# Attention: full softmax weights kept in PSUM over their scores, and their sum split between GpSimd and TensorE

## The chip, the cores and the metric

The kernel runs on one core of one Trainium2 chip. The metric is the device time of one launch in microseconds (us). The core has TensorE for matrix products (PE in the rows, PEld for its weight loads), VectorE (DVE), ScalarE (ACT), GpSimd (POOL) and SyncE (SP), which only issues DMAs here. Each engine takes its instructions strictly in the order in which they were built and waits on semaphores for the others.

## The reference

One step of a four-layer network over 1024 latent and 128 context tokens of 1024 channels: Hyena, latent attention (MLA), RWKV-7, Hyena. The change touches the attention of the second layer alone. For each of 16 heads it computes

```
s = einsum('bqhd,bkhd->bhqk', qn, k_nope) + einsum('bqhr,bkr->bhqk', qp, k_pe)
p = softmax(s * 96 ** -0.5, axis=-1)
o = einsum('bhqk,bkhd->bqhd', p, v)          # then  (o * silu(z)) @ w_out
```

where the 1024 latent queries see 1280 keys (256 cached, 1024 own) and the 128 context queries see 128 keys. Head width is 64 plus 32 positional channels, values are 64 wide.

## The kernel before, in words

Products are made at nearly full precision from split operands: a value x is kept as a rounded high part and a low part x - high, and a product is high*high + high*low + low*high.

Scores are computed transposed, keys on partitions and queries on columns, in **tiles** of 128 keys by 512 queries. A head has 21 tiles: ten key blocks for queries 0 to 511, ten for queries 512 to 1023 (each ten is a **group**), and one small tile, 128 by 128, for the context. For a tile, `scores` issues three products into a PSUM bank (L1459 to L1461). The first has a 97th row, which subtracts each query's maximum. `attend` then lets ScalarE read the bank twice: `exp` in full into a tile `pf` (L1492, for the first tile of a group straight into the sum `sm`) and `exp` rounded into `wh` (L1493). VectorE subtracts them into the low part `wl` (L1497), GpSimd adds `pf` to the group's running sum `sm` (L1499). `values` multiplies both parts with the values, [v_hi | v_lo] side by side in 128 columns, into one bank `ps_pv` (L1466, L1467). Tiles `pf`, `wh` and `wl` come from rings of four, so that ScalarE can be four tiles ahead of the last reader of a ring.

`finish` follows each group: the low half of `ps_pv` is copied (L1517) and added to the high half (L1519), the columns of `sm` are summed over partitions on TensorE (L1523), inverted (L1525), spread, transposed (L1534) and multiplied in with the gate (L1536, L1537).

Beside head h run `maxima(h + 1)` and `head_prep(h + 2)`. `maxima` takes 25 products of queries by keys (L1436, eight times 512, 512 and 256 columns, once 128), each reduced to row maxima on VectorE (L1437), then L1440 and L1441, a transpose (L1443), a copy `mr` on ScalarE (L1445), and a DMA that writes the maxima into row 96 of the queries `qh` (L1446). No score of a head can start before that DMA has landed. `head_prep` makes keys, queries and values of later heads (L262 to L264 into `ps_pj`, with ScalarE copies and VectorE subtractions).

PSUM has eight banks. In this stage `set_banks` gives three in turn to maxima and projections (`pj`), one to `fn`, two to the scores (`st`) and two to `pv`. A scheduler sets the order of instructions on each engine when the kernel is built; the steps of `weave` are only its input.

Of the kernel before, what the change touches and what calls it, by code (L numbers as in the profile page):

```python
# [20 lines left out]
P = 128  # L21
# [111 lines left out]
def rwkv_constants():  # L133
# [19 lines left out]
    # of each level's mask the columns that change, for four chunks of each direction  # L153
# [69 lines left out]
class Prog:  # L223
# [22 lines left out]
    def set_banks(self, **kinds):  # L246
        """Which PSUM banks each kind of product (or several kinds together) takes, in turn."""
# [22 lines left out]
    def load_split(self, hi, lo, src, lo_eng=None, pool=None):  # L270
        """DRAM [1024, n <= 128] -> split [128, KC, n], through a staging tile, in two halves."""
# [18 lines left out]
    def mod_part(self, i, part):  # L290
        """Columns (part * 512 ...) of silu(cond) @ mod_w[i] + mod_b[i], for both conditions."""
# [40 lines left out]
    def mod_fast(self, i):  # L332
        """Shift and scale of both conditions on the tensor engine; 16 steps."""
# [30 lines left out]
    def fold_mod(self, i):  # L364
        """h = xn * G + B with xn the normalised rows (or x itself before the first layer)."""
# [21 lines left out]
    def next_group(self, i):  # L387
        """Room for another group of tokens of layer i's input; the RWKV layer takes it unsplit."""
# [6 lines left out]
    def emit_h(self, i, t, xn, pool):  # L395
        """Token tile t of xn (token-major) -> modulated, channel-major, split in hh / hl (or in h32)."""
# [72 lines left out]
    def load_w(self, src):  # L469
        """src [1024, 128]: split weights, k-chunks along the free axis."""  # L470
# [26 lines left out]
    def boundary(self, i, w_out, y_src, last):  # L497
        """x <- LN(alpha x + gate * (y @ w_out)); y_src(t) loads token tile t as [128, KC, 128], split."""
# [3 lines left out]
        with tc.tile_pool(name="bd", bufs=1, reuse_waits="tile") as pool:  # L502
# [23 lines left out]
            def load_x(t):  # L526
                """alpha x, kept as that after the first layer."""
# [66 lines left out]
    def wout_half(self, w_out, half, turns=True):  # L594
        """Half the columns of w_out, split, in a pool at the far end of the memory; four steps."""
# [11 lines left out]
    def norm_stats(self, s, pool):  # L607
        """Mean and 1 / deviation of every row, in columns 0 and 2."""
# [12 lines left out]
    def load_cst(self, r, k, pool, bufs, raw=False):  # L621
        """DFT constants, split; from the given ones the first time."""
# [14 lines left out]
    def fw_mats(self, r, t):  # L637
        """(re->re, im->re, re->im, im->im) as (hi, lo) pairs."""
# [3 lines left out]
    def stage1_odd(self, xo, out, pool, w):  # L642
        """Odd outputs of the 16-point DFT of eight values; out(r, part)."""
# [4 lines left out]
        # real  # L648
# [14 lines left out]
        # imaginary  # L663
# [16 lines left out]
    def stage1_even(self, xe, out, pool, w):  # L680
        """Even outputs of the 16-point DFT of eight values."""
# [31 lines left out]
    def stage1_inv(self, u, out, pool, w):  # L713
        """u(r, part) -> out(a), a in 0..7 (the inverse of the residues)."""
# [87 lines left out]
    def sine(self, ps, w, freq, fb, y, k):  # L802
        """sin(freq * ps + fb) with the argument reduced to [-pi, pi]."""
# [12 lines left out]
    def features(self, j, pool, fd):  # L816
        """Hidden features of the implicit filter at all positions, split, one block for each pair of taps."""
# [42 lines left out]
    def filters(self, j, pool):  # L860
        """Spectra of the two-sided filter (plus the skip at lag 0), unit by unit -> DRAM."""
# [14 lines left out]
        def weights(q):  # L876
            """Output weights of the filter network, decays and skip of unit q."""
# [91 lines left out]
    def hyena(self, i, j, lead, rest):  # L969
        """lead: steps that come before the first product with h; rest: steps to be done by the end."""  # L970
# [12 lines left out]
        def conv3(col, dst, then):  # L983
            """Job: three-tap convolution of u column tile `col` into dst() [128, W] (a spare column at LS)."""
# [46 lines left out]
        def jobs_gate(b):  # L1031
            """conv3(x0) * silu(z) -> DRAM."""
# [29 lines left out]
        def blocks(q, pool):  # L1062
            """Time blocks of v * x1, token-major."""
# [133 lines left out]
    def mla(self, i, rest):  # L1197
        """rest: steps to be done by the end."""
# [42 lines left out]
        def latents():  # L1241
            """Queries' and keys' compressed forms, token-major -> normalised, channel-major, split."""
# [61 lines left out]
        def early():  # L1304
            """What needs no room of the layer's input."""
# [25 lines left out]
        def pair_values(p):  # L1331
            """Values of a pair of heads, token-major: [v_hi | v_lo] of each head side by side."""
            wk, vv = pairs[p][0], self.big([P, NK, 2, 2, 64], "vv")
            pairs[p].append(vv)
            for t0 in range(0, NK, 4):
                n = min(4, NK - t0)
# [6 lines left out]
                dst = vv[:, t0:t0 + n].rearrange("p t a b n -> p t (a b) n")  # L1343
                nc.scalar.copy(dst[:, :, 0:4:3], src)
                nc.vector.tensor_tensor(dst[:, :, 1:3], src, dst[:, :, 0:4:3], ALU.subtract)
# [16 lines left out]
        def turn(u):  # L1362
            """Positional parts of the queries of four heads, 32 rows each."""
# [28 lines left out]
        def head_prep(h):  # L1392
            """Keys and queries of a head."""
# [55 lines left out]
        rings = [[self.mp.tile([P, 512], F32, tag=tag, name="pf", bufs=n) for tag, n in  # L1449
                  (("macc0", 1), ("macc1", 1), ("modw", 2), ("modw", 2))]]  # L1450
# [13 lines left out]
        def values(h, t, first, last, pv, ph, pl, done):  # L1464
            vl = pairs[h // 2][1][:, t, h % 2].rearrange("p a n -> p (a n)")
            nc.tensor.matmul(pv, vl, ph, start=first, stop=False)  # L1466
            nc.tensor.matmul(pv, vl, pl, start=False, stop=last)  # L1467
            if last:
                later.append([1, finish(h, *done)])

        def attend():
            """All heads' softmax and weighted values, 42 steps each."""
# [3 lines left out]
            due = []  # L1476
            for i, (h, q0, nq, t, first, last) in enumerate(tiles):
                if h % 2 and first:
# [11 lines left out]
                if first:  # L1490
                    pf = sm
# [70 lines left out]
        for x in later:  # L1562
            weave(x[1])
# [770 lines left out]
```

## Time and profile before

| what | before |
|---|---|
| median of three runs | 4658.84 us (4657.1 to 4663.7) |
| span of the profiled execution, first to last instruction | 4633.9 us |
| between that span and the median of the runs | 24.9 us |
| attention stage, 1160 to 1856 us of the span: PE, DVE, ACT, POOL busy | 649.1, 647.8, 463.0, 546.0 of 696 us |
| granted TensorE clock in the stage | 0.97 of full speed |

The span is what the trace covers; the time of a run is a little longer. Busy time of PE overlaps itself (ends of products are modelled), so PE is read by the distance between starts.

### The profile page before, as it was taken

The page shows a single profiled execution, that of the slowest core. Times are in us where ns is not written, and L with a number is a line of the kernel's source. Part 1 is how long each engine was busy: PE and PEld are TensorE (multiplying, and loading weights), DVE is VectorE, ACT ScalarE, POOL GpSimd, SP SyncE. Part 2 cuts the span into 40 slices and gives each one's busy share as a digit, 9 for nine tenths or more (in the row PEclk, how much of TensorE's full clock was granted, in tenths as well). Part 3 has the DMA queues.
Part 4 walks back from the last instruction along what each step waited for, and adds up shares of the span by engine and source line. Part 5 has one row for each costly group of instructions (what it writes and reads, how often), then busy time and mean ns, then how long its engine had stood idle before and what let it go on. Part 6 is the DMA issues. An engine that isn't in the chain of part 4 may idle for free. (4 is left out here: it accounts for less than half of the span.)

```text
span 4633.9 us, 81733 instructions
## 1 busy us (share of the span) xinstructions
PE 4125.1 (89%) x29736; PEld 3562.3 (77%) x29736; DVE 3545.7 (77%) x6307; ACT 2395.0 (52%) x5468; POOL 2358.6 (51%) x1902
## 2 busy tenths in 40 slices
PE   7988988989999998978989777999999889988998
PEld 4888888778777776767877566888888678978986
DVE  6777887655999999587578996777777568967877
ACT  5654433554676676344455544666566456643331
POOL 3655766343787787355546652233333233476550
PEclk8999999988999999989978886999899899989999
DMA  5755455543000001436635462222222423764445
GB/s 174 241 181 174 156 158 171 185 135 98 18 17 24 26 15 39 137 130 196 176 116 184 163 228 74 59 79 71 77 72 65 136 95 113 222 202 151 144 151 181
DMA packets 490975, 582.90 MB, mean 126 GB/s; under 512 B 59819, under 2 KB 378333, under 8 KB 489933
## 3 DMA queue, kind: packets, MB, share of 16 engines
q1 hardware_dynamic: 489068, 576.70, 39.7%
q8 instruction: 235, 3.85, 0.3%
q14 instruction: 168, 1.37, 0.1%
q10 hardware_dynamic: 1504, 0.98, 0.1%
HBM read 413.74 MB, written 161.37 MB: 124 GB/s over the span
## 5 line engine op out<-in xcount | busy, mean ns | idle before, releaser
L262 PE MATMUL ps_mm<-hh,wh 128*128 128x384 f32 x1728 | 594.3, 345 | 47.6 <-ACT hh L267 24.0
L263 PE MATMUL ps_mm<-hl,wh 128*128 128x384 f32 x1728 | 592.8, 343 | 2.6 <-DVE hl L268 1.6
L264 PE MATMUL ps_mm<-hh,wl 128*128 128x384 f32 x1728 | 591.8, 343 | 0.0
L1499 POOL TENSOR_TENSOR sm<-sm,pf 128x512 f32<-128x512 f32 x288 | 443.1, 1539 | 115.4 <-DVE wl L1497 37.3
L268 POOL TENSOR_TENSOR wl<-wraw,wh 128x512 fp32r<-128x512 f32 x212 | 331.2, 1580 | 182.5 <-ACT wh L267 170.1
L262 PEld LDWEIGHTS ps_mm<-hh,wh 128*128 128x128 f32 x1728 | 334.0, 194 | 56.2 <-ACT hh L267 25.1
L1497 DVE TENSOR_TENSOR wl<-pf,wh 128x512 fp32r<-128x512 f32 x288 | 352.1, 1232 | 7.9 <-ACT wh L1493 7.6
L263 PEld LDWEIGHTS ps_mm<-hl,wh 128*128 128x128 f32 x1728 | 333.9, 193 | 7.6 <-DVE hl L268 4.3
L264 PEld LDWEIGHTS ps_mm<-hh,wl 128*128 128x128 f32 x1728 | 333.8, 193 | 3.3 <-issue 3.3
L2139 POOL TENSOR_TENSOR tot<-SV,wcs 64x128 f32<-64x128 f32 x288 | 114.7, 405 | 391.6 <-DVE SV L2167 360.6
L305 POOL TENSOR_TENSOR macc<-macc,mprod 128x512 f32<-128x512 f32 x140 | 212.3, 1517 | 172.3 <-ACT mprod L304 139.6
L263 PE MATMUL ps_mm<-mx,wh 128*128 128x384 f32 x680 | 254.6, 375 | 35.1 <-DVE mx L1669 34.0
L262 PE MATMUL ps_mm<-mx,wh 128*128 128x384 f32 x680 | 257.3, 380 | 13.9 <-ACT mx L1668 5.7
L262 PE MATMUL ps_mm<-woh,hh 128*128 128x512 f32 x576 | 235.8, 411 | 33.8 <-ACT hh L267 31.0
L264 PE MATMUL ps_mm<-mx,wl 128*128 128x384 f32 x680 | 249.3, 368 | 3.7 <-POOL wl L268 3.7
L1492 ACT ACTIVATE pf<-ps_st 128x512 f32<-128x512 f32 x288 | 172.4, 599 | 143.4 <-POOL sm L1499 57.5
L264 PE MATMUL ps_mm<-woh,hl 128*128 128x512 f32 x576 | 234.5, 407 | 2.9 <-DVE hl L268 2.8
L263 PE MATMUL ps_mm<-wol,hh 128*128 128x512 f32 x576 | 232.2, 403 | 0.1
L1437 DVE TENSOR_REDUCE mx<-ps_pj 128x1 f32<-128x512 f32 (+2 forms) x400 | 220.0, 574 | 13.4 <-PE ps_pj L1436 12.6
L302 DVE SCALAR_TENSOR_TENSOR macc<-modw,cond,macc 128x512 f32<-128x512 f32 x140 | 156.4, 1118 | 92.8 <-DMA modw<-mod_w 92.1
L304 ACT ACTIVATE mprod<-modw,cond 128x512 f32<-128x512 f32 x140 | 101.3, 724 | 197.3 <-POOL macc L305 109.3
L1493 ACT ACTIVATE wh<-ps_st 128x512 fp32r<-128x512 f32 x336 | 194.3, 578 | 0.0
(560 smaller groups left out, 13314.6 us busy)
## 6 DMA issues: line engine op xcount, KB each, us to landing
cst<-cst SPq DMA_DIRECT2D x175, 384.0 KB
modw<-mod_w SPq DMA_DIRECT2D x160, 256.0 KB
wraw<-hy_w_in SPq DMA_DIRECT2D x128, 256.0 KB
kd<-kt SPq DMA_DIRECT2D x72, 384.0 KB
kt<-kd SPq DMA_DIRECT2D x72, 384.0 KB
cst<-cst SPq DMA_DIRECT2D x41, 512.0 KB
ctd<-ct SPq DMA_DIRECT2D x24, 768.0 KB
bkd<-bk SPq DMA_DIRECT2D x24, 768.0 KB
```

The source lines that it names most:

```text
L262: mm(ps, lh, rh, start=start, stop=False)
L263: mm(ps, lh, rl, start=False, stop=False)
L264: mm(ps, ll, rh, start=False, stop=stop)
L268: (lo_eng or self.nc.gpsimd).tensor_tensor(lo, src, hi, ALU.subtract)
L302: nc.vector.scalar_tensor_tensor(acc[0], w, s, acc[0], op0=ALU.mult, op1=ALU.add)
L305: nc.gpsimd.tensor_tensor(acc[1], acc[1], wp, ALU.add)
L1437: nc.vector.tensor_reduce(mx[:, t, j:j + 1], ps, AX.X, ALU.max)
L1492: nc.scalar.activation(pf, s, AF.Exp, scale=scale)
L1493: nc.scalar.activation(ph, s, AF.Exp, scale=scale)
L1497: nc.vector.tensor_tensor(pl, pf, ph, ALU.subtract)
L1499: nc.gpsimd.tensor_tensor(sm, sm, pf, ALU.add)
L2139: g_.tensor_tensor(tot[h], SV[e][h, jsl], wc[h].unsqueeze(2).broadcast_to([64, 2, 64]), M)
```

## The change

The full weights are no longer written to SBUF. ScalarE writes the rounded weights `wh` first and then overwrites the scores in their own PSUM bank with the full weights; VectorE subtracts `wh` from that bank. The ring of `pf` goes. GpSimd's running sum adds the rounded parts `wh` only. The sum of the low parts comes from TensorE: the values get 32 columns of ones between their parts (288 columns a key block for two heads: lo, hi, ones, hi, lo), and the product of the low part takes hi and ones, while that of the high part takes lo and hi. The two products now accumulate in two PSUM regions, `a` and `b`. `finish` copies both halves of `a` (L1543, L1544), copies the row of ones' sums (L1546), adds `b` on VectorE (L1547), and two more additions on GpSimd join the sums (L1549) and the output (L1550). The last key block's values live in a small tile of their own (`vl`). Banks are dealt anew: maxima, projections and `fn` share two, the scores have three, `pv` three.

```diff
-            wk, vv = pairs[p][0], self.big([P, NK, 2, 2, 64], "vv")
+            wk, vp = pairs[p][0], self.big([P, NK - 1, 288], "vv")
+            last = self.mp.tile([P, 1, 288], F32R, tag=f"macc{p % 2}", name="vl", bufs=1)
...
+                nc.gpsimd.tensor_copy(x[:, :, 128:160], self.ones[:, :32].unsqueeze(1).broadcast_to([P, n, 32]))
...
-                nc.vector.tensor_tensor(dst[:, :, 1:3], src, dst[:, :, 0:4:3], ALU.subtract)
+                for e in range(2):
+                    nc.vector.tensor_tensor(dst[:, :, e * 224:e * 224 + 64], src[:, :, e], hi[:, :, e], ALU.subtract)
...
-            nc.tensor.matmul(pv, vl, ph, start=first, stop=False)
-            nc.tensor.matmul(pv, vl, pl, start=False, stop=last)
+            nc.tensor.matmul(g["a"], pairs[h // 2][1][t][:, c0:c0 + P], ph, start=first, stop=last)
...
+            nc.tensor.matmul(g["b"], pairs[h // 2][1][t][:, c0:c0 + P], pl, start=first, stop=last)
...
-                nc.scalar.activation(pf, s, AF.Exp, scale=scale)
-                nc.scalar.activation(ph, s, AF.Exp, scale=scale)
+                    nc.scalar.activation(ph, s, AF.Exp, scale=scale)
+                    nc.scalar.activation(s, s, AF.Exp, scale=scale)
...
-                nc.vector.tensor_tensor(pl, pf, ph, ALU.subtract)
-                if not first:
-                    nc.gpsimd.tensor_tensor(sm, sm, pf, ALU.add)
+                    nc.vector.tensor_tensor(pl, s, ph, ALU.subtract)
...
+                        nc.gpsimd.tensor_tensor(g["sm"], before if t == 1 else g["sm"], p32, ALU.add)
...
-            nc.scalar.copy(au[mrow], pv[arow])
+            nc.scalar.copy(au[mrow], g["a"][arow])
+            nc.scalar.copy(oT[mrow, qs], g["a"][mrow])
...
-            nc.vector.tensor_tensor(oT[mrow, qs], pv[mrow], au[mrow], ALU.add)
+            nc.scalar.copy(au[srow], g["b"][srow])
+            nc.vector.tensor_tensor(au[mrow], g["b"][mrow], au[mrow], ALU.add)
+            yield False
+            nc.gpsimd.tensor_tensor(sm[srow], sm[srow], au[srow], ALU.add)
+            nc.gpsimd.tensor_tensor(oT[mrow, qs], oT[mrow, qs], au[mrow], ALU.add)
...
-        self.set_banks(pj=(0, 1, 2), fn=(5,), st=(3, 4), pv=(6, 7))
+        self.set_banks(pj_fn=(0, 1), st=(2, 3, 4), pv=(5, 6, 7))
```

The scheduler also orders the stage differently. First place: TensorE at the end of the sixth head, before the change, from the head's last scores (the small tile). L1443 is the transpose of the next head's maxima; the next head's first scores stand six rows behind this piece.

```order
L1459 MATMUL ps_st<-qh,kh_10355 128x128
L1460 MATMUL ps_st<-qh,kh_10355 128x128
L1461 MATMUL ps_st<-qh,kh_10355 128x128
L1466 MATMUL ps_pv<-wh,vv 128x512
L1443 MATMUL ps_pj<-ident,mn 9x128
L1467 MATMUL ps_pv<-wl,vv 128x512
L1466 MATMUL ps_pv<-wh,vv 128x512
L1467 MATMUL ps_pv<-wl,vv 128x512
L1523 MATMUL ps_fn<-ones,sm 128x1 x4
L1466 MATMUL ps_pv<-wh,vv 128x128
L262 MATMUL ps_pj<-qTh,wqu 128x384
L263 MATMUL ps_pj<-qTl,wqu 128x384
```

The same place after the change, from the eleventh row behind the head's last scores on. L1441 is the product of the maxima (L1436 before), L1448 their transpose, L1554 the sums of `sm`; the next head's first scores (L1463) stand eight rows behind this piece.

```order
L1441 MATMUL ps_pj<-kh_10353,qh 128x512 x2
L1441 MATMUL ps_pj<-kh_10353,qh 128x256
L1441 MATMUL ps_pj<-kh_10353,qh 128x512 x2
L262 MATMUL ps_pj<-cTh,wku 64x384
L263 MATMUL ps_pj<-cTl,wku 64x384
L264 MATMUL ps_pj<-cTh,wku 64x384
L1441 MATMUL ps_pj<-kh_10353,qh 128x256
L1441 MATMUL ps_pj<-kh_10353,qh 128x512 x2
L1441 MATMUL ps_pj<-kh_10353,qh 128x128
L1441 MATMUL ps_pj<-kh_10353,qh 128x256
L1554 MATMUL ps_fn<-ones,sm 128x1 x4
L1448 MATMUL ps_pj<-ident,mn 9x128
```

Before, all products of the next head's maxima stood ahead of the head's last scores; now thirteen of the 25 stand behind them (three of these ahead of the piece), and the transpose behind those.

Second place: VectorE at the end of the same head after the change. L1518 is the subtraction of weights (L1497 before), L1442 the reduction of a maxima product, L1547 the addition of `finish`, L1445 and L1446 the last steps of the maxima.

```order
L1518 TENSOR_TENSOR wl<-ps_st,wh 128x512
L1442 TENSOR_REDUCE mx<-ps_pj 128x1
L1518 TENSOR_TENSOR wl<-ps_st,wh 128x128
L1442 TENSOR_REDUCE mx<-ps_pj 128x1 x2
L1547 TENSOR_TENSOR au<-ps_pv,au 64x512
L1547 TENSOR_TENSOR au<-ps_pv,au 64x128
L1442 TENSOR_REDUCE mx<-ps_pj 128x1 x6
L1394 TENSOR_TENSOR kh_10354<-ps_pj,kh_10354 64x384
L1442 TENSOR_REDUCE mx<-ps_pj 128x1 x3
L1446 TENSOR_SCALAR mn<-mx 128x1
L1442 TENSOR_REDUCE mx<-ps_pj 128x1
L1445 TENSOR_REDUCE mn<-mx 128x8
```

Before, the steps L1440 and L1441 of the next head's maxima stood ahead of the subtraction of the small tile; now twelve reductions follow it.

## Rows read from the trace of the kernel before

**Rows 1.** The page's busy time, its share of the span and instructions of each engine.

```profile
PE 4125.1 (89%) x29736; PEld 3562.3 (77%) x29736; DVE 3545.7 (77%) x6307; ACT 2395.0 (52%) x5468; POOL 2358.6 (51%) x1902
```

**Rows 2.** Windows: length, PE, PEld, DVE, ACT, POOL busy, clock, DMA share, GB/s.

```profile
1160.00:1856.00 696.00, 649.08 (x2994) 497.61 (x2992) 647.83 (x940) 462.95 (x932) 545.99 (x379) 0.97 0.08 24
```

**Rows 3.** Instructions of line L1459: duration min/median/max, first and last start.

```profile
L1459 PE MATMUL ps_st<-qh,kh x336: 222/398/774, 1158.3 to 1850.9; 97*128 97x512 f32 x160, 97*128 97x128 f32 x8
```

**Rows 4.** Groups by form, DVE, 1160 to 1856: count | busy us, mean ns | idle.

```profile
L1497 DVE TENSOR_TENSOR wl<-pf,wh 128x512 fp32r<-128x512 f32 x288 | 352.1, 1232 | 7.9 <-ACT wh L1493 7.6
...
L1497 DVE TENSOR_TENSOR wl<-sm,wh 128x512 fp32r<-128x512 f32 x32 | 25.6, 800 | 1.6 <-ACT wh L1493 1.2
...
L1389 DVE TENSOR_TENSOR kh<-ps_pj,kh 64x512 fp32r<-64x512 f32 x28 | 18.9, 675 | 6.8 <-ACT kh L1388 6.8
```

**Rows 5.** Timeline, DVE, 1357 to 1361: start us, duration us.

```profile
1357.06 0.67 DVE L1497 TENSOR_TENSOR wl<-sm,wh 128x512 fp32r<-128x512 f32 x1
1357.66 0.67 DVE L1497 TENSOR_TENSOR wl<-pf,wh 128x512 fp32r<-128x512 f32 x1
...
1358.93 0.67 DVE L1519 TENSOR_TENSOR oT<-ps_pv,au 64x512 f32<-64x512 f32 x1
...
1360.12 2.16 DVE L1497 TENSOR_TENSOR wl<-pf,wh 128x512 fp32r<-128x512 f32 x1
```

**Rows 6.** Timeline, POOL, the same stretch.

```profile
1357.87 1.63 POOL L1499 TENSOR_TENSOR sm<-sm,pf 128x512 f32<-128x512 f32 x1 [2.49 <-ACT q L1412]
1359.46 1.01 POOL L268 TENSOR_TENSOR qh<-qe,qh 96x384 fp32r<-96x384 f32 x1
1360.44 1.29 POOL L1499 TENSOR_TENSOR sm<-sm,pf 128x512 f32<-128x512 f32 x1
```

**Rows 7.** Groups by form, POOL, 1160 to 1856.

```profile
L1499 POOL TENSOR_TENSOR sm<-sm,pf 128x512 f32<-128x512 f32 x288 | 443.1, 1539 | 115.4 <-DVE wl L1497 37.3 <-ACT pf L1492 36.3 <-DVE ri L1525 11.9
```

**Rows 8.** Groups by form, ACT, 1160 to 1856.

```profile
L1492 ACT ACTIVATE pf<-ps_st 128x512 f32<-128x512 f32 x288 | 172.4, 599 | 143.4 <-POOL sm L1499 57.5 <-PE ps_st L1461 43.0 <-issue 26.5
```

**Rows 9.** Waits, 1160 to 1856: us in total, times, longest us.

```profile
PEld ps_pv L1467 <- DVE wl L1497: 83.8, 127, 2.6
...
PEld ps_pj L1436 <- DVE mx L1437: 9.7, 26, 1.2
```

**Rows 10.** Timeline, PE, around the ends of heads: start us, duration us.

```profile
1197.70 0.23 PE L1459 MATMUL ps_st<-qh,kh 97*128 97x128 f32 x1
...
1201.76 0.44 PE L1459 MATMUL ps_st<-qh,kh 97*128 97x512 f32 x1
...
1283.07 0.23 PE L1459 MATMUL ps_st<-qh,kh 97*128 97x128 f32 x1
...
1290.21 0.27 PE L1443 MATMUL ps_pj<-ident,mn 128*9 128x128 f32 x1
...
1293.79 0.50 PE L1459 MATMUL ps_st<-qh,kh 97*128 97x512 f32 x1
...
1294.36 0.39 PE L1461 MATMUL ps_st<-qh,kh 96*128 96x512 f32 x1
1294.59 0.40 PE L1459 MATMUL ps_st<-qh,kh 97*128 97x512 f32 x1
...
1810.61 0.22 PE L1459 MATMUL ps_st<-qh,kh 97*128 97x128 f32 x1
...
1817.25 0.77 PE L1459 MATMUL ps_st<-qh,kh 97*128 97x512 f32 x1
```

**Rows 11.** Timeline, DVE, at the head's end of 1283 us.

```profile
1288.99 0.15 DVE L1441 TENSOR_SCALAR mn<-mx 128x1 f32<-128x1 f32 x1
```

**Rows 12.** Timeline, ACT, at the same head's end.

```profile
1284.51 0.30 ACT L1493 ACTIVATE wh<-ps_st 128x128 fp32r<-128x128 f32 x1
...
1291.40 0.26 ACT L1445 CAST mr<-ps_pj 9x128 fp32r<-9x128 f32 x1
```

**Rows 13.** Timeline, SP (its DMA issues), at the same head's end.

```profile
1291.69 0.79 SPq L1446 DMA_DIRECT2D qh<-mr  x1
```

More of the change, by code (lines that the diff above doesn't have):

```diff
@@ L1331, in pair_values @@
         def pair_values(p):
[L1333 to L1336 removed]
+            wk, vp = pairs[p][0], self.big([P, NK - 1, 288], "vv")
+            last = self.mp.tile([P, 1, 288], F32R, tag=f"macc{p % 2}", name="vl", bufs=1)
+            pairs[p].append([vp[:, t] for t in range(NK - 1)] + [last[:, 0]])
+            for x in (vp, last):
+                n = x.shape[1]
+                nc.gpsimd.tensor_copy(x[:, :, 128:160], self.ones[:, :32].unsqueeze(1).broadcast_to([P, n, 32]))
+            for t0, n in ((0, 4), (4, 4), (8, 2), (NK - 1, 1)):
                 ps = self.psum("pj")
@@ L1448, in mla @@
         later = []
-        rings = [[self.mp.tile([P, 512], F32, tag=tag, name="pf", bufs=n) for tag, n in
-                  (("macc0", 1), ("macc1", 1), ("modw", 2), ("modw", 2))]]
+        rings = []
         for tag in ("wh", "wl"):
@@ L1462, in scores, with values_hi, values_lo @@
             return s
-        def values(h, t, first, last, pv, ph, pl, done):
-            vl = pairs[h // 2][1][:, t, h % 2].rearrange("p a n -> p (a n)")
-            nc.tensor.matmul(pv, vl, ph, start=first, stop=False)
-            nc.tensor.matmul(pv, vl, pl, start=False, stop=last)
-            if last:
-                later.append([1, finish(h, *done)])
+        def values_hi(g, t, first, last, ph):
+            h, nq = g["h"], g["nq"]
+            if first:
+                bank = self.psum("pv")
+                g["a"] = bank[:, :nq]
+                if nq == P:
+                    g["b"] = bank[:, P:2 * P]
+            c0 = h % 2 * 160
+            nc.tensor.matmul(g["a"], pairs[h // 2][1][t][:, c0:c0 + P], ph, start=first, stop=last)
+            if last:
+                later.append(finish(g))
+        def values_lo(g, t, first, last, pl):
+            h, nq = g["h"], g["nq"]
+            if "b" not in g:
+                g["b"] = self.psum("pv")[:, :nq]
+            c0 = 64 + h % 2 * 32
+            nc.tensor.matmul(g["b"], pairs[h // 2][1][t][:, c0:c0 + P], pl, start=first, stop=last)
         def attend():
@@ new lines, in attend @@
+            his, los = [], []
+            for i in range(len(tiles) + 3):
+                if i < len(tiles):
+                    h, q0, nq, t, first, last = tiles[i]
+                    if h % 2 == 0 and q0 == 0 and first:
+                        oT = outs[:, h // 2 % 2]
+                        ri = pool2.tile([P, 2, NT], F32, tag="ri", name="ri", bufs=2)
+                    if first:
+                        sz = None
+                        if h % 2:
+                            sz = pool2.tile([P, 512], F32, tag="szl", name="szl", bufs=2)[:, :nq]
+                            nc.sync.dma_start(sz, szd[h // 2, :, q0:q0 + nq])
+                        g = dict(h=h, q0=q0, nq=nq, sz=sz, oT=oT, ri=ri,
+                                 sm=pool2.tile([P, 512], F32, tag="sm", name="sm", bufs=3)[:, :nq])
+                    s = ahead.pop(0)
+                    ph, pl = (x[i % 4][:, :nq] for x in rings)
+                    nc.scalar.activation(ph, s, AF.Exp, scale=scale)
+                    nc.scalar.activation(s, s, AF.Exp, scale=scale)
+                if his:
+                    values_hi(*his.pop(0))
+                if len(los) > 1 or (los and i >= len(tiles)):
+                    values_lo(*los.pop(0))
+                yield
+                if i < len(tiles):
+                    nc.vector.tensor_tensor(pl, s, ph, ALU.subtract)
+                    p32 = ph.bitcast(F32)
+                    if first and last:
+                        nc.gpsimd.tensor_copy(g["sm"], p32)
+                    elif not first:
+                        nc.gpsimd.tensor_tensor(g["sm"], before if t == 1 else g["sm"], p32, ALU.add)
+                    before = p32
+                    if i + 2 < len(tiles):
+                        ahead.append(scores(*tiles[i + 2]))
+                    his.append((g, t, first, last, ph))
+                    los.append((g, t, first, last, pl))
@@ L1503, in attend, with finish @@
                 for x in list(later):
-                    x[0] -= 1
-                    if x[0] < 0 and next(x[1], True):
+                    if next(x, True):
                         later.remove(x)
-                if last and q0 == LS:
+                if i < len(tiles) and last and q0 == LS:
                     del qhs[h]
                 yield
-            values(*due.pop())
-        def finish(h, q0, nq, pv, sm, sz, oT, ri):
+        def finish(g):
+            h, q0, nq, sm, sz, oT, ri = (g[x] for x in ("h", "q0", "nq", "sm", "sz", "oT", "ri"))
```

31 lines of the change are left out of this document (6 added, 25 removed).

## The prediction

> **What bounds the kernel now.** The page comes first: PE is busy in 89% of the span and nothing else in more than 77% [rows 1], so the whole kernel has no single bound and the change must be judged in its stage. The attention lies between the first and the last scores, 1158.3 and 1850.9 us [rows 3]: 692.6 us, 43.3 a head. There the windows show PE at 649 and DVE at 648 of 696 us, POOL at 546, ACT at 463 [rows 2]. PE's busy time overlaps itself. Full-size products start 0.23 us apart, as at 1294.36 and 1294.59 [rows 10], and by that distance (in proportion for narrower ones, 0.11 for those of 128 columns) all products between first and last scores sum to 559 us: PE has over 130 us to spare. DVE has none to speak of, and PE waits for it: 83.8 us for `wl` in the longest wait [rows 9].
>
> Why DVE is full stands in the groups by form. The subtraction of weights takes 1232 ns on average, while a subtraction of the same width that takes one operand from PSUM takes 675 [rows 4]. The timelines show what lengthens it: at 1357.66 it takes 0.67 us, and GpSimd's addition which starts inside it ends late (1.63 against 1.29). At 1360.12 it starts inside GpSimd work, lasts 2.16 us, and ends half a microsecond after the next GpSimd addition has ended at 1361.73; the VectorE addition from PSUM at 1358.93 keeps its 0.67 beside both [rows 5, 6]. So a subtraction with two SBUF operands and a GpSimd addition exclude each other, and one with a PSUM operand does not.
>
> The stage has a second part: between a head's last scores and the next head's first. These gaps last 4.06 us at the first of 15 heads' ends and 6.64 at the last, 10.72 at the longest but one that I follow here [rows 10]; together 83.0 us. Hence 609.6 us, or 38.1 a head, are spent between first and last scores of heads.
>
> **The change, part by part.** *The subtraction* now reads PSUM: 288 times 1232 becomes 675, 32 times 800 becomes 675 [rows 4], 164 us less DVE work. *GpSimd's additions* go from 1.54 [rows 7] to 1.29 [rows 6] and 0.08 us of handover, 48 us less; but `finish` brings two full-width ones for each of 32 groups, at 1.29 (a row of one partition is priced as a full one, bounds 0.1 and 1.3), and small ones for the 16 context tiles: 100 us more with the ones. GpSimd so comes to 600 us, 37 a head. *ScalarE* gets 37 us of copies, hidden in 233 idle us [rows 2]; if that cover were gone they would cost 2.3 us a head. Overwriting scores in PSUM is not in the trace; I take the 0.6 us of the exp into SBUF [rows 8], bounds 0.5 and 0.7, which by 320 is 32 us either way on an engine that does not set the pace. *TensorE* does as many products of the same sizes. *Values' subtractions* come in two pieces: under 5 us on DVE, in its freed time. *Banks and order* are what is left, and they move the most.
>
> Steady part. Between first and last scores of heads the new order leaves PE 458 us of products (28.3 in most heads, 32.3 in three, less in the last two) instead of 507, because products of the maxima moved out. Before, 507 us of products took 609.6, a ratio of 0.83, under a full DVE. After, DVE needs 22 us a head there, ScalarE at most 25, GpSimd about 28 until its ring lets the last scores go, so PE with 28.3 is the longest, and three engines lie close behind it. I take a ratio of 0.92; bounds 0.88 (in-order engines waiting on two banks) and 1. That gives 498 us (458 to 520), **112 us less** than 609.6.
>
> Gaps. Of the 375 products for maxima of heads 1 to 15, the order before left 12 behind the previous head's last scores; the order after leaves 182, nine to fourteen in every gap. As no score starts before the maxima's DMA lands, that work lies bare. The chain for the sixth head, whose order stands above: from last scores to the end of the small tile's exp, 1.74 us as at 1283 [rows 10, 12]. Then VectorE, at 0.60 us from start to start for 512 columns [rows 5]: the small subtraction 0.2, twelve reductions (seven of 512, four of 256, one of 128) 5.6, additions and the keys 1.25, last steps 0.15; 7.2. Then waits for the two banks, 1.0: a keys' product holds one of them for about 1.7 us through product, copy and subtraction, while the other goes on. Then transpose, `mr`, DMA, scores: at 1283 this took 4.65 us from the end of L1441 and 3.58 from the transpose [rows 10, 11], through `mr` at 1291.40 and the DMA's issue at 1291.69 [rows 12, 13]; behind the sums' products I take 3.9. Sum 13.8 us. Seven of the gaps hold a values' product, more keys and queries as well and get 15; the last two, with nine maxima, 14 and 11. Together 6 x 13.8 + 105 + 25 = 213 us (180 to 240 for 12 to 16 a gap), **130 us more** than 83.
>
> So the stage takes 498 + 213 = 711 us instead of 692.6: 18 more. Outside it, orders differ in single swaps. The profiled span goes from 4633.9 to 4652, and with the 24.9 us around it that the median of 4658.8 shows, the time to 4677.
>
> Against this stands a rule. The Trainium skill (Perfetto Trace Analysis, Identifying the Most-Contended Engine) says to take the engine with the highest occupancy for the bottleneck, and to relieve it first. VectorE is that engine here besides TensorE [rows 2], so by this rule the change gains; the first rival prices it. The same page (Optimization Strategy) says that a gap that repeats can mean too little room in SBUF or PSUM for the next tile; the trace has such a repeating gap [rows 10], and by this sentence fewer banks for the maxima widen it.
>
> **Rivals.** *VectorE's relief comes through.* The gaps close faster than my chain, because the reductions drain while exps of the last tiles still run and the two banks cost nothing. Place: the gap from last to first scores; it decides where the mean gap falls under (692.6 - 498) / 15 = 13.0 us. At 12 us, and a steady ratio of 0.96 (477), the stage takes 657: the time is 4623. With gaps at 13 and the same ratio, 672: 4638. For it: 164 us leave a full engine, and the longest wait of PE is for it. Against it: the 4.65 us tail is measured, and DVE work in a gap is 8.3 to 10.7 us by count. Chance 0.30.
>
> *No change to be seen.* The two sums cancel within 9 us (0.2%, about what a measurement of this kernel can tell from no change). Chance 0.18.
>
> *Bare gaps and the two banks, as forecast.* Gaps 13.5 to 16, steady ratio 0.90 to 0.93: 4668 to 4705, likeliest 4677. Chance 0.42.
>
> *The clock falls in the gaps.* In them PE has 6 to 9 us of products in 14. The stage has 0.97 of full speed now [rows 2], and the scores at 1817.25, right after a gap, take 0.77 us against 0.40 [rows 10], half speed. If that followed every gap for some 5 us of products, each would cost 2 to 3 us more, 40 us in all: 4700 to 4720. Against it: the gap of 10.72 us ended at full speed (0.23 from start to start). Chance 0.07.
>
> *The subtraction is held up by GpSimd as before*, with one SBUF operand too: then the steady part keeps 610 us and the gaps come on top, 4659 + 130 = 4789. The row at 1358.93 speaks against it. Chance 0.03.
>
> **How the numbers follow.** Faster takes the first rival, 0.30; same 0.18; slower the last three, 0.52. The likeliest is the forecast, 4677, with its own range of 4668 to 4705. The range over all cases leaves out a tenth at either side: below, steady 0.97 with gaps of 12 (652 us, 4618) is the edge of the first rival, so 4622; above, the clock's 4720.
>
> **What would show it.** In the trace after: L1518 of 512 columns near 675 ns on average (right) or over 1000 (the last rival). The distance from the 128-column row of L1463 to the next full one: 13 to 16 us (right), under 13 (first rival); scores right behind it 0.43 us apart (clock). From first to last scores 700 to 730 us. POOL near 600 us in the stage, with additions near 1.3 us; if they stay at 1.54, GpSimd needs some 41 us a head and comes near to setting the pace itself. The forecast would be wrong most easily in the steady ratio: 0.04 of it is 20 us, more than the whole difference.

## The result, and the profile after

The changed kernel takes 4789.03 us (median of 4 runs, 4776.51 to 4800.77) against 4659.61: a ratio of 1.0277, 95% interval 1.0257 to 1.0296. It is slower, as forecast, but by 129 us instead of 18, outside the range.

The page's busy times of the changed kernel, whose span is 4782.3 us, to be read beside [rows 1]:

```profile
PE 4235.1 (89%) x29736; PEld 3651.5 (76%) x29736; DVE 3421.5 (72%) x6347; ACT 2439.8 (51%) x5572; POOL 2370.7 (50%) x2030
```

Windows of the same kernel (columns as in [rows 2]): the stretch from the first to the last scores; then the gap behind the sixth head, the seventh head, and the gap behind it:

```profile
1179.00:1978.30 799.30, 731.76 (x2994) 566.95 (x2995) 514.42 (x974) 503.77 (x1027) 548.06 (x494) 0.84 0.07 22
...
1471.53:1488.65 17.12, 13.49 (x47) 9.30 (x45) 11.10 (x24) 5.21 (x14) 9.22 (x11) 0.70 0.00 0
1488.65:1523.56 34.91, 34.65 (x177) 29.12 (x175) 23.77 (x44) 24.67 (x49) 27.29 (x24) 1.00 0.10 29
1523.56:1549.02 25.46, 19.11 (x62) 12.06 (x61) 13.06 (x30) 7.54 (x20) 11.71 (x13) 0.62 0.12 36
```

VectorE has 514 us of work where it had 648 [rows 2], and the stage takes 107 us more all the same. TensorE's granted clock fell from 0.97 to 0.84 of full speed: whole (2.4 GHz) inside the seventh head, 0.70 and 0.62 on average in the gaps around it, where it stood at its half level (1.2 GHz) for part of the time.

The groups by form of VectorE and of GpSimd in that stretch, two of each, answer to [rows 4, 7]:

```profile
L1518 DVE TENSOR_TENSOR wl<-ps_st,wh 128x512 fp32r<-128x512 f32 x319 | 218.8, 687 | 125.7 <-ACT ps_st L1511 119.3 <-PE ps_pv L1487 2.6 <-PE ps_st L1465 1.2
L1442 DVE TENSOR_REDUCE mx<-ps_pj 128x1 f32<-128x512 f32 x238 | 159.1, 684 | 37.6 <-PE ps_pj L1441 35.4
```

```profile
L1523 POOL TENSOR_TENSOR sm<-sm,wh 128x512 f32<-128x512 f32 x253 | 327.1, 1293 | 38.3 <-ACT wh L1510 24.5
...
L1549 POOL TENSOR_TENSOR sm<-sm,au 1x512 f32<-1x512 f32 x31 | 39.8, 1285 | 8.8 <-ACT au L1546 6.7
```

The subtraction fell to 687 ns and GpSimd's addition to 1293, both as forecast. But VectorE now stands idle for 120 us ahead of L1518, waiting for ScalarE. The waits of TensorE (us in total, times, longest) name what is late. A wait of the products (PE) lies inside that of their weight load (PEld), so the two lines of a pair are not added. The wait for `wl` that led before, 83.8 us [rows 9], has shrunk to 2.4:

```profile
PEld ps_pj L1441 <- DVE mx L1442: 65.4, 88, 2.5
...
PE ps_pj L1441 <- DVE mx L1442: 33.9, 54, 2.3
```

Products of the maxima wait for a bank that a reduction still reads. Before, that wait was 9.7 us [rows 9].

The table gives the parts of the profiled execution of each kernel, from the starts of the scores' products in its trace. "Lead" is the time from the last transposes of the keys (L1310) to the first scores; "heads" and "gaps" together are the stage; in brackets the maxima's products in the gaps; "rest" is what follows the last scores.

| kernel | banks: maxima + sums, scores, values | lead | heads | gaps | stage | rest |
|---|---|---|---|---|---|---|
| before | 3 + 1, 2, 2 | 77 | 609.6 | 83.0 (27) | 692.6 | 2783 |
| changed | 2 shared, 3, 3 | 97 | 518.6 | 280.7 (190) | 799.3 | 2804 |
| e1 changed, banks of before | 3 + 1, 2, 2 | 90 | 658.4 | 20.7 (12) | 679.1 | 2804 |
| e2 before, banks of the change | 2 shared, 3, 3 | 80 | 642.1 | 265.8 (162) | 907.9 | 2797 |
| e3 a score bank idle | 2 shared, 2, 3 | 95 | 593.7 | 133.6 (44) | 727.3 | 2786 |
| e4 maxima early | 2 shared, 3, 3 | 97 | 770.4 | 23.8 (7) | 794.3 | 2818 |
| e5 relief alone | 3 + 1, 2, 2 | 79 | 618.2 | 29.4 (21) | 647.6 | 2817 |
| e6 no sums | 3 + 1, 2, 2 | 78 | 540.7 | 75.2 (41) | 615.9 | 2788 |
| e7 another deal | 3 shared, 3, 2 | 90 | 510.9 | 129.3 (60) | 640.2 | 2810 |
| e8 maxima twice | 2 shared, 3, 3 | 99 | 549.9 | 301.3 (195) | 851.1 | 2802 |
| e9 = e7, values apart | 3 shared, 3, 2 | 81 | 505.3 | 142.8 (65) | 648.2 | 2807 |
| e10 before again | 3 + 1, 2, 2 | 79 | 609.7 | 81.6 (27) | 691.4 | 2780 |
| e11 a value bank idle | 2 shared, 3, 2 | 94 | 516.5 | 265.2 (182) | 781.7 | 2808 |
| e12 = e11, TensorE kept busy | 2 shared, 3, 2 | 104 | 633.5 | 284.8 (174) | 918.3 | 2780 |
| e13 = e9, maxima early | 3 shared, 3, 2 | 75 | 546.9 | 105.8 (40) | 652.7 | 2809 |

The 148 us between the two spans are thus 107 in the stage, 21 ahead of it (19 of them in the lead) and 21 behind it, where nothing is changed. The last sum is not tied to the change: e10, which is the kernel before, takes 2780 us there, but so does e12, a form of the changed kernel. e10 also shows that a run (4644.1 us) lasts 1.8 us longer than its span (4642.3). So the profiled execution of the kernel before was some 24 us shorter than the median of its runs, and most of the 24.9 us that the prediction put outside the span was this distance. The profiled execution of the changed kernel was 5 us shorter than its median; that is why the medians differ by 129 us and the spans by 148.

### The profile page after: what moved, and what is told of

It reads as the page before. It is cut to its first block, busy times and chain, and to the rows that moved or that the text cites. A ratio compares the mean times of both kernels' runs of the same rounds, so it can differ in the third digit from the quotient of the medians.

```text
span 4782.3 us, 81992 instructions
## 1 busy us (share of the span) xinstructions
PE 4235.1 (89%) x29736; PEld 3651.5 (76%) x29736; DVE 3421.5 (72%) x6347; ACT 2439.8 (51%) x5572; POOL 2370.7 (50%) x2030
## 5 line engine op out<-in xcount | busy, mean ns | idle before, releaser
L1523 POOL TENSOR_TENSOR sm<-sm,wh 128x512 f32<-128x512 f32 x256 | 330.9, 1293 | 38.4 <-ACT wh L1510 24.5
L1518 DVE TENSOR_TENSOR wl<-ps_st,wh 128x512 fp32r<-128x512 f32 x336 | 223.9, 668 | 126.3 <-ACT ps_st L1511 119.8
L1442 DVE TENSOR_REDUCE mx<-ps_pj 128x1 f32<-128x512 f32 (+2 forms) x400 | 226.2, 583 | 71.7 <-PE ps_pj L1441 68.5
L1441 PE MATMUL ps_pj<-kh,qh 96*128 96x512 f32 (+2 forms) x400 | 177.2, 473 | 53.6 <-DVE mx L1442 42.6
```

Source lines behind the costliest of these rows:

```text
L1441: nc.tensor.matmul(ps, qh[:96, 0, t * P:(t + 1) * P], kh[:96, 0, c0:c0 + n], start=True, stop=True)
L1442: nc.vector.tensor_reduce(mx[:, t, j:j + 1], ps, AX.X, ALU.max)
L1518: nc.vector.tensor_tensor(pl, s, ph, ALU.subtract)
L1523: nc.gpsimd.tensor_tensor(g["sm"], before if t == 1 else g["sm"], p32, ALU.add)
```

## The experiments

The theory to begin with was the prediction's: the loss is the place of the maxima, behind each head's last scores. The rivals: the additions that the new sums need, the two banks wherever the maxima stand, and the clock.

**e1: the banks of before.**

```diff
-        self.set_banks(pj_fn=(0, 1), st=(2, 3, 4), pv=(5, 6, 7))
+        self.set_banks(pj=(0, 1, 2), fn=(5,), st=(3, 4), pv=(6, 7))
```

> The changed kernel with the banks dealt as before (three for maxima and projections, one for the sums, two for the scores, two for the weighted values); everything else as changed. By the theory that the loss is the order that the new deal brings (maxima behind the head's last scores), 12 maxima stand behind last scores instead of 190, the gaps between heads come to some 80 us instead of 281, and with VectorE relieved the stretch from first to last scores of heads takes about 560 us (507 us of products over 0.9) instead of 610: 4600 us, 4570 to 4640, faster than before. By the rival that the additions which the new sums need (GpSimd, ScalarE, two accumulations) cost the time, it stays above 4700 whatever the banks are.

4658.19 us, ratio 1.001 (0.9991 to 1.0029): the whole loss goes with the deal of banks, but the hoped gain does not come. The gaps nearly vanish, but the heads take 658 us instead of the expected 560. Waits of TensorE in the stage of e1 show a new one; before, no wait of the scores for VectorE is among the longer ones:

```profile
PEld ps_st L1463 <- DVE wl L1518: 35.9, 78, 1.2
...
PE ps_st L1463 <- DVE wl L1518: 10.9, 23, 1.0
PEld ps_pj L1441 <- DVE mx L1442: 8.8, 17, 1.3
```

Scores wait for the subtraction, because a score bank is now free only when VectorE has read it: 36 us in all, against 1.4 us in the changed kernel, where the scores have a third bank. My reading had no term for it.

**e2: the new deal alone, in the kernel before.**

```diff
-        self.set_banks(pj=(0, 1, 2), fn=(5,), st=(3, 4), pv=(6, 7))
+        self.set_banks(pj_fn=(0, 1), st=(2, 3, 4), pv=(5, 6, 7))
```

> The kernel before with the new deal of banks alone (two for maxima, projections and sums, three for scores, three for weighted values). By the theory of the order, 201 maxima come to stand behind last scores, the gaps grow from 83 to some 280 us at about half the clock, and what moves out shortens the rest from 610 to about 510; with 20 us more ahead of the first scores: 4780, 4740 to 4830. By the rival that the arithmetic of the change costs the time, within 30 us of the kernel before.

4867.77 us, ratio 1.0448 (1.0425 to 1.0471), more than expected. It also came about in another way: 162 maxima stand behind last scores, not 201, the gaps take 266 us for 280, and the heads take 642 us where 510 were expected. With e1 it makes a square of stages: with the banks of before 692.6 us become 679.1 by the rest of the change, with the new banks 907.9 become 799.3. The rest of the change gains 14 and 109 us; the deal costs 215 and 120.

**e3: the third score bank unused.**

```diff
-        self.set_banks(pj_fn=(0, 1), st=(2, 3, 4), pv=(5, 6, 7))
+        self.set_banks(pj_fn=(0, 1), st=(2, 3), pv=(5, 6, 7))
```

> The changed kernel with its third bank for scores left unused: maxima, projections and sums keep their two banks, scores get two, weighted values three, and one bank holds nothing. 44 maxima stand behind last scores instead of 190. By the theory that the third bank for scores lets these run ahead of the maxima in the order, the gaps fall to 100 to 150 us and the time to 4630 to 4700, though a bank less is used. By the rival that two banks are too few for the maxima wherever they stand, the time stays at 4750 or more, with a longer stretch between first and last scores instead of the gaps.

4710.51 us, ratio 1.0112 (1.0081 to 1.0144), some 10 us above the first band and 40 below the second. A bank less is 72 us better in the stage, although the maxima have the same two banks and scores now wait 21 us for the subtraction. In most heads of e3 the maxima stand singly or in twos and threes between scores; the three heads that keep eleven behind their last scores have the longest gaps, 19 us each. The Trainium skill (Perfetto Trace Analysis, Matmul Optimizations) advises to make use of all eight PSUM banks; here a kernel that uses seven beats one that uses eight, so their number alone does not decide.

**e4: the maxima woven in earlier, banks as changed.**

```diff
-NM = 52
+NM = 200
```

> The changed kernel with its banks, but the steps of the maxima woven in four times as fast, so that only 7 of them stand behind last scores. By the theory of the order, the gaps fall to 60 to 100 us, the stretch from first to last scores takes 560 to 590 us (507 of products over 0.88), the 20 us ahead of the first scores stay: 4610 to 4670. By the rival that two banks cannot feed the maxima beside a head, TensorE waits at them inside the heads instead, and the time stays above 4720.

4790.38 us, ratio 1.0272 (1.0235 to 1.0309). It is not the place behind last scores by itself that costs: 7 products instead of 190 stand there, the gaps fall to 23.8 us, and the heads take nearly all of it back (770.4). But e4 does not spread the maxima out either. In ten of its heads twelve to fourteen of them stand in one bunch between the starts of the 17th and the 18th scores, and these ten stretches last 18 to 21 us each, as long as gaps of the changed kernel. One of them (columns as in [rows 2]):

```profile
1510.39:1531.24 20.85, 17.64 (x60) 12.17 (x59) 12.30 (x26) 4.91 (x11) 4.64 (x4) 0.61 0.00 1
```

So e4 moved the bunch four tiles forward. The same two waits of TensorE as in the changed kernel, now inside the heads of e4:

```profile
PEld ps_pj L1441 <- DVE mx L1442: 90.1, 130, 1.5
...
PE ps_pj L1441 <- DVE mx L1442: 43.8, 77, 0.8
```

**e5: the relief of VectorE alone, in the kernel before.**

```diff
-        rings = [[self.mp.tile([P, 512], F32, tag=tag, name="pf", bufs=n) for tag, n in
-                  (("macc0", 1), ("macc1", 1), ("modw", 2), ("modw", 2))]]
+        rings = []
...
-                nc.scalar.activation(pf, s, AF.Exp, scale=scale)
                 nc.scalar.activation(ph, s, AF.Exp, scale=scale)
+                nc.scalar.activation(s, s, AF.Exp, scale=scale)
...
-                nc.vector.tensor_tensor(pl, pf, ph, ALU.subtract)
-                if not first:
-                    nc.gpsimd.tensor_tensor(sm, sm, pf, ALU.add)
+                nc.vector.tensor_tensor(pl, s, ph, ALU.subtract)
+                p32 = ph.bitcast(F32)
...
+                    nc.gpsimd.tensor_tensor(sm, before if t == 1 else sm, p32, ALU.add)
+                before = p32
```

> The kernel before with one part of the change: the full weights overwrite their scores in PSUM, VectorE subtracts from there, and GpSimd sums the rounded weights (the sum of the low parts is left out). Banks, values and the end of a group stay as before. VectorE gets some 150 us lighter here. By the theory that a score bank, now held until the subtraction has read it instead of until the second exp, is what the relief is paid with (two banks for the scores), the time stays within 30 us of the kernel before: 4630 to 4680, with TensorE's scores waiting for the subtraction. By the rival that VectorE's relief is worth its time where the banks are not touched, 4560 to 4610.

4614.78 us, ratio 0.9923 (0.9898 to 0.9949), between the two bands: the relief pays 45 us of stage, and scores wait for the subtraction here too (52 us). Against e1, which has the same banks, the stage is 31 us shorter. What e1 has beyond e5 is above all the two accumulations and the longer end of a group; that these cost the 31 us is not shown, since no run takes them one by one.

**e6: no sums on GpSimd, in the kernel before.**

```diff
-                if not first:
-                    nc.gpsimd.tensor_tensor(sm, sm, pf, ALU.add)
+                if last and not first:
+                    nc.vector.tensor_scalar(sm, sm, 1.0, None, op0=ALU.add)
```

> The kernel before without GpSimd's additions of the full weights (a group's sum is its first tile plus one, so that it can be inverted). The subtraction keeps its two SBUF operands, and the score banks come free at the second exp as before. By the theory that the subtraction and GpSimd's additions exclude each other, it falls from 1232 ns to 660 to 700 on average. With VectorE so relieved and the banks as before, the attention should take 590 to 640 us of 693: 4560 to 4610. If VectorE was not what the stage waited for, the subtraction gets short and the time stays above 4640.

4565.65 us, ratio 0.9831 (0.9788 to 0.9875). VectorE's group of the subtraction in e6, beside 1232 ns in [rows 4]:

```profile
L1497 DVE TENSOR_TENSOR wl<-pf,wh 128x512 fp32r<-128x512 f32 x287 | 205.6, 721 | 34.4 <-ACT wh L1493 31.3 <-PE ps_st L1461 1.8
```

Two SBUF operands are still there, GpSimd's additions are not, and the subtraction is short (721 ns, a little above the expected 700); so it was the pair that excluded each other. The Trainium skill (SBUF — State Buffer, SBUF: two separate sides) says that VectorE and GpSimd share one pair of ports, which one instruction holds alone; this row agrees. The stage is 77 us shorter. Not all of that is VectorE's relief: the run also takes 443 us of work off GpSimd [rows 7], and with it the 57.5 us that ScalarE waited for GpSimd's sums [rows 8].

**e7: three banks for maxima and sums, three for scores, two for values.**

```diff
-        self.set_banks(pj_fn=(0, 1), st=(2, 3, 4), pv=(5, 6, 7))
+        self.set_banks(pj_fn=(0, 1, 2), st=(3, 4, 5), pv=(6, 7))
```

> The changed kernel with its eight banks dealt in another way: three for maxima, projections and sums, three for the scores, two for the weighted values. By the theory that two banks cannot feed maxima, projections and sums (first deal), and two cannot feed scores that are held until the subtraction (second deal), this one takes 620 to 660 us in the stage: 4590 to 4640, faster than before. By the rival that two accumulations need three banks, TensorE waits for the end of each group and the time stays at 4660 to 4720.

4631.94 us, ratio 0.9957 (0.9937 to 0.9976): as expected, and faster than both kernels, if only by 0.4% than the one before.

**e8: each product of the maxima twice.**

```diff
                     nc.tensor.matmul(ps, qh[:96, 0, t * P:(t + 1) * P], kh[:96, 0, c0:c0 + n], start=True, stop=True)
+                    nc.tensor.matmul(ps, qh[:96, 0, t * P:(t + 1) * P], kh[:96, 0, c0:c0 + n], start=True, stop=True)
```

> The changed kernel with every product of the maxima issued twice into its bank, so that TensorE has more to do between heads. If TensorE's clock, which was 0.67 to 0.7 of full speed in the gaps, is a main price of the gaps, it rises above 0.85 there and the gaps fall from 281 us to 200 to 260. If the two banks and the reductions set their pace, they grow by 190 products of 0.23 to 0.45 us, to 310 to 370 us, whatever the clock does, and the time to 4820 to 4880.

4857.45 us, ratio 1.0443 (1.0407 to 1.0479), gaps of 301.3 us at a mean clock of 0.73: between the bands for the gaps, and the clock did not come back. So it doesn't tell what a whole clock would be worth. It does show that TensorE has time to spare in the gaps: a second product of each costs only 0.1 us there (21 us over 195).

**e9: e7, and the last key block's values in tiles of their own.**

```diff
-            last = self.mp.tile([P, 1, 288], F32R, tag=f"macc{p % 2}", name="vl", bufs=1)
+            last = pool2.tile([P, 1, 288], F32R, tag=f"vl{p % 2}", name="vl", bufs=1)
```

> The deal of e7 (three for maxima, projections and sums, three for scores, two for values), and the last key block's values in tiles of their own instead of the two that the next layer's modulation sums in until shortly before the attention. In e7 and in the changed kernel ScalarE waits for that modulation with its copy into the small values tile, and the first head's maxima stand behind. By the theory that this wait is what the first scores lose, they begin 75 to 85 us after the last transposes of the keys, as before (77), instead of 90, the rest is as in e7, and the time is 4600 to 4630. If the first scores are late for another reason, 88 us or more, and the time of e7, 4632.

4620.87 us, ratio 0.9931 (0.9906 to 0.9955), and the lead falls from 90 to 81 us, as expected. The stage is 8 us longer than that of e7. The wait that it removes stands in the changed kernel's timeline of ScalarE (start and duration in us, in brackets the idle time before and what ended it):

```profile
1152.66 0.27 ACT L1348 CAST vl<-ps_pj 128x128 fp32r<-128x128 f32 x1 [1.75 <-PE ps_ax L314]
1155.43 0.40 ACT L267 CAST wqu<-wqr 128x256 fp32r<-128x256 f32 x1 [2.51 <-PE ps_pj L263]
```

The copy into `vl` waits for the next layer's modulation (L314), whose tile it takes over; queries queue behind it on ScalarE.

**e10: the kernel before once more.**

> The kernel before, unchanged, once more with a profile. It tells how far two profiles of one kernel differ outside the attention: from the last scores to the end the profile of before took 2783 us, those of the other kernels 2786 to 2818, though nothing is changed there. By the theory that this is a spread between executions, this one lies anywhere in 2783 to 2820 and its attention takes 690 to 695 us.

A stage of 691.4 and a rest of 2780 us, below the expected 2783 to 2820. The stage repeats to 1.2 us and the rest to 3; the first scores start 12.5 us later (1170.8 against 1158.3). So this run by itself doesn't show the spread behind the stage; e12 does, which is as short there.

**e11 and e12: a bank left idle, and TensorE kept busy with it.** e11:

```diff
-        self.set_banks(pj_fn=(0, 1), st=(2, 3, 4), pv=(5, 6, 7))
+        self.set_banks(pj_fn=(0, 1), st=(2, 3, 4), pv=(5, 6))
```

> The changed kernel with two banks for the weighted values instead of three, and one bank unused; beside it stands the next run. 182 maxima stand behind last scores instead of 190. If two banks are enough for the two accumulations, the stage takes 790 to 820 us, as the changed kernel's 799; if not, above 830.

A stage of 781.7 us (4774.2 in one run), below the first band: two banks are enough for the values. That makes e7 a change of one bank, the idle one given to the pool of maxima, projections and sums: 781.7 becomes 640.2 us. TensorE's waits for a maxima bank, in e11:

```profile
PEld ps_pj L1441 <- DVE mx L1442: 49.5, 79, 1.4
...
PE ps_pj L1441 <- DVE mx L1442: 23.2, 48, 0.8
```

and in e7:

```profile
PEld ps_pj L1441 <- DVE mx L1442: 6.6, 13, 1.5
...
PE ps_pj L1441 <- DVE mx L1442: 2.3, 3, 1.1
```

e12 adds to e11:

```diff
+                    old = mx.rearrange("p t j -> p (t j)")[:, 3 * t + j - 2:3 * t + j - 1]
+                    for x in range(3 if 3 * t + j > 1 else 0):
+                        nc.tensor.matmul(hot[0][:1, x * P:(x + 1) * P], old, self.ident, start=True, stop=True)
...
-        self.set_banks(pj_fn=(0, 1), st=(2, 3, 4), pv=(5, 6))
+        self.set_banks(pj_fn=(0, 1), st=(2, 3, 4), pv=(5, 6), hot=(7,))
+        hot.append(self.psum("hot"))
```

> The run before this one with three small products (128 columns) of the maxima's reductions into the unused bank behind each product of the maxima; nobody reads them. They wait for no bank, so TensorE has work in the gaps where it waited. If the half clock is a main price of the gaps, it rises above 0.9 there and the gaps fall by 40 to 100 us against the run before, though 500 more products stand in them. If the two banks and the reductions set the pace, the gaps stay within 20 us of the run before or grow, at whatever clock.

4892.99 us in one run. The clock came back, 0.98 in the gaps on average where e11 has 0.72, and the gaps took 285 us against 265. By the expectation that favours the banks; but some 470 small products stand in these gaps, and those within heads cost 0.2 us each (117 us more for some 560), so they may hide a gain. The clock's own share stays open.

**e13: e9 with the maxima woven in earlier.**

```diff
-NM = 52
+NM = 104
```

> The kernel of e9 (three banks for maxima, projections and sums) with the steps of the maxima woven in twice as fast, so that 40 of them stand behind last scores instead of 65. With two banks, an earlier place only moved the time from the gaps into the heads (e4: 794 us in the stage, as 799). If the place of the maxima is worth something once three banks feed them, the gaps fall from 143 to 80 to 110 us, the heads grow by less, and the stage takes 600 to 630 us: 4575 to 4605. If the place is worth nothing there either, the heads take what the gaps give: 640 to 655 us in the stage, 4610 to 4635.

4627.07 us, ratio 0.9943 (0.9928 to 0.9958). The gaps give 37 us and the heads take 42: with three banks, this earlier place is worth nothing.

## Why the prediction was right or wrong, step by step

**Right.** The subtraction (687 ns for 675), GpSimd's addition (1293 for 1.29 us), its one-row addition priced as a full one (1285), and the exp in place (594 ns for 0.6). The heads took 518.6 us, at the far end of 458 to 520: the ratio was 458 / 518.6 = 0.88, its lower bound. The reductions behind last scores were where the order put them; counted by the products' starts in the trace they are 190 in the gaps (27 before), not the 182 and 12 of the text. GpSimd came to 548 us in the stage, not 600, in part because its additions took their 1.29 us with no handover of 0.08 on top.

**Where the 112 us went that were missed.** 68 are the gaps, 20 the heads, 21 lie ahead of the first scores and 21 behind the last; 18 go off again, since the median lies 7 us above the profiled span here and not 24.9. The forecast's own range of 4668 to 4705 was also narrower than its bounds: 13.5 us a gap with a ratio of 0.93 gives 4661, 16 with 0.90 gives 4715. The 4789 of the last rival, which is the measured time to the microsecond, is luck: its sign, L1518 over 1000 ns, did not come.

**Wrong in size: the gaps, 281 us instead of 213.** The sixth head's gap, worked out at 13.8 us, took 17.1. Its rows on VectorE:

```profile
1473.88 0.28 DVE L1518 TENSOR_TENSOR wl<-ps_st,wh 128x128 fp32r<-128x128 f32 x1
...
1475.70 0.90 DVE L1547 TENSOR_TENSOR au<-ps_pv,au 64x512 f32<-64x512 f32 x2 [0.61 <-POOL vl L1338]
...
1478.52 1.29 DVE L1442 TENSOR_REDUCE mx<-ps_pj 128x1 f32<-128x512 f32 x2 [0.26 <-PE ps_pj L1441]
1480.73 0.42 DVE L1442 TENSOR_REDUCE mx<-ps_pj 128x1 f32<-128x256 f32 x1 [0.93 <-PE ps_pj L1441]
...
1484.47 0.18 DVE L1445 TENSOR_REDUCE mn<-mx 128x8 f32<-128x24 f32 x1
```

and on TensorE:

```profile
1477.38 0.38 PE L1441 MATMUL ps_pj<-kh,qh 96*128 96x256 f32 x1 [1.48 <-DVE mx L1442]
...
1479.26 0.58 PE L262 MATMUL ps_pj<-cTh,wku 128*64 128x384 f32 x1 [0.31 <-DVE mx L1442]
...
1480.28 0.41 PE L1441 MATMUL ps_pj<-kh,qh 96*128 96x256 f32 x1
...
1488.65 0.52 PE L1463 MATMUL ps_st<-qh,kh 97*128 97x512 f32 x1
```

The first and last parts came out: scores 4.0 us behind the end of L1445, for 3.9. The middle failed: from the end of the small exp to that of L1445 it took 11.4 us for 8.2. VectorE was busy for 8.9 us of it, for 7.2; it reached the small subtraction only 0.6 us after the small exp, behind a reduction that stood ahead of it. It was idle for 2.5 us, for the 1.0 of "waits for the two banks": 0.6 ahead of L1547 and 1.7 in four waits for products of the maxima (0.26, 0.93, 0.31, 0.22), which themselves waited for the banks that its reductions free. So "waits for the two banks, 1.0" and the 7.2 of VectorE's work were both mis-sized, by half of the 3.2 us each. The gaps with a values' product, put at 15, took up to 25.5; what makes these longest ones is not worked out here.

**Half right in cause.** The forecast charged the place of the maxima, bare behind last scores. That the deal of banks brings the loss is shown: e1 gives the old deal back and the loss goes, e2 brings the new one into the kernel before and the stage grows by 215 us, and one bank more for the maxima's pool (e7 against e11) takes 142 us off it. But behind last scores is not the only bad place: e4 has the maxima in one bunch inside the head, and pays the same. And the number of their banks is not all: e3 leaves them two, has most of them spread over the head, and its stage is 72 us shorter. So the runs point to the bunch, wherever it stands; on three banks too the three gaps of e7 that hold eleven or twelve maxima are its longest, 14.4 to 18.6 us. The deal decides whether the scheduler's order makes such bunches: e7 leaves 60 maxima behind last scores where e11 leaves 182. What the third bank is worth by itself, in an order that stays as it is, no run shows. What the first rival counted on, VectorE's relief, does pay where the banks are not touched: 45 us of stage in e5.

**Not seen at all.** The lead, where the text had "single swaps": 19 us, 9 of them `vl` (e7 to e9); perhaps 4 more go with e7's other bank (94 in e11, 90 in e7), though the lead of the kernel before alone differs by 1.7 between two executions. And the hold of a score bank through the subtraction, which e1 pays with 36 us of waits and the changed kernel, with three score banks, with 1.4.

**The clock**, a rival with 0.07, did fall, in every gap (0.62 to 0.79 on average). In the sixth head's gap it stood at 1.00 up to 1478.5 us, about a microsecond after TensorE's wait of 1.48 us shown above, and at 0.50 from there to the next scores. What it costs can be read from pairs of gaps with the same products. In e9 the gaps behind the third and the eleventh head hold the same 60, but for four that stand elsewhere in the order, at a whole and at a lowered clock:

```profile
1277.90:1293.37 15.47, 12.31 (x61) 8.72 (x59) 10.47 (x25) 8.98 (x24) 11.68 (x14) 1.00 0.20 60
1615.90:1634.51 18.61, 16.55 (x62) 12.46 (x61) 10.09 (x24) 9.30 (x23) 10.11 (x12) 0.72 0.17 49
```

That is 3.1 us for one gap. The same two gaps of e7 differ by 1.7 us (14.4 at 1.00, 16.1 at 0.79), and two gaps of e8 with all products in the same order by 1.9 (17.1 at 0.86, 19.0 at 0.65). The rival had 2 to 3. For fifteen gaps 1.7 to 3.1 us would be an estimate of 26 to 47 us, of the 68 that the gaps took beyond the forecast; no run here shows it by itself.

## What to carry to other kernels

Before making an engine lighter by letting results stay in PSUM, count how long each bank is held, from its first product to its last reader: eight banks are shared out among all kinds of products, and what one kind gains another loses. Where an order leaves work bare in one bunch, look at what another order does to the bunch: e4 only moved it and gained nothing, e3 spread it out and gained 72 us, and with a third bank (e7) the scheduler built an order with fewer and smaller bunches. A tile that takes over the room of a neighbouring stage also takes over its waits.

## What the runs showed that was not expected

The part behind the attention, the same in all kernels, takes 2780 to 2818 us, so differences under 40 us outside a changed stage can't be read from two profiles. Its length goes with the clock granted in it: 0.90 of full speed in the two profiles of the kernel before and in e12 (2780 to 2783 us), 0.88 in e4 (2818). A product issued twice into its bank cost 0.1 us in a gap (e8), where full-size ones otherwise start 0.23 apart. And a bank that holds nothing did no harm: e11 was 18 us shorter in the stage than the kernel that used it.
